# Sixteen weight fetches moved up behind the mixture's branch, the last eight of them on POOL's queue

## The chip, the cores and the metric

One core of a Trainium2 chip runs the whole program in one launch. The metric is device time in microseconds (us), the median of several executions. TensorE is called PE, VectorE DVE, ScalarE ACT, GpSimd POOL and SyncE SP, as in the profile.

## The reference, cut to what matters

Two blocks run one behind the other on 256 tokens of width 1024. The first block has two layers; each is an attention part and then a mixture of experts. The second block (two layers of feed-forward, a three-branch mixer and feed-forward) is untouched by the change. The mixture, with 16 experts of width 1024 and 2 experts per token:

```python
expert, gate = route(h, w_router, b_router)         # 2 of 16 experts for each token
def expert_block(args):
    xblk, e = args
    return (jax.nn.silu(xblk @ w_gate[e]) * (xblk @ w_up[e])) @ w_down[e]
...
y = yb.reshape(n_pad, D) * slot_gate[:, None].astype(h.dtype)
return jnp.zeros_like(h).at[slot_tok].add(y)
```

Everything is fp32. One expert has three 1024 x 1024 matrices of 4 MB, so a layer's mixture reads 16 x 3 x 4 MB = 192 MB of weights, each byte once.

## The kernel before, in words

The mixture is `moe`, called once for each layer. It takes every expert with room for CAP = 64 tokens, two experts (a pair, `pr` = 0 to 7) beside each other in the array. For a pair it forms three products: gate, up and down (`product`, L1883). Between them stand the activation (L1899), the multiplication of gate and up (L1911), eight transposes (L1920), and, behind the down product, four small matmuls for each half that scatter the result back to the tokens (L1951, added up by DVE at L1955).

The weights come in tiles of 1 MB (128 partitions of 8 KB), numbered `n` from 0 to 191 in the order in which they are used: 24 a pair, eight each for gate, up and down. A product has four steps `u`, and a step uses two tiles, one for each expert. `fetch(n)` (L1750) takes a slot from a ring of 16 (`e.wst` with 14 and `wst2` with 2) and issues one DMA on SP's queue (L1762); the last tiles go in smaller parts (L1769, L1776). A tile may be fetched as soon as the tile 16 before it has been used, so the ring always holds the next 16 tiles. The waits are generated, not written: a fetch waits for its slot, and for the landing of an earlier DMA that used the same of SP's completion semaphores.

An expert may get more than 64 tokens. For that there is a general path, `moe_overflow` (L1975), in a branch on the largest count (L1979). Every engine comes past that branch; with these inputs no engine goes into it. It stands in pair 5 behind the transposes, that is ahead of pair 5's down product. Just ahead of it, 16 fetches are issued in a loop (tiles 136 to 151: pair 5's down and pair 6's gate), so that the ring is full when the engines come to the branch. All later fetches are asked for where a product needs its tile (`if i not in loaded: fetch(i)` in `product`).

The order of the instructions on each engine is set by a planner, which takes the program's order as priority and estimates when each instruction could run; it also decides which free slot a tile gets. Nothing from outside is put into the branch.

Behind the branch, the first layer also loads the memory's keys and values of the second layer (`mem_kv`, L1280 and L1285: tiles `mkvT`, `mkv`; 1 MB ahead of the branch, 2 MB behind it), and PE forms them in two groups of 32 matmuls (L1292 and L1299). In the first layer, too, POOL's next instruction behind the branch is the load of the table `rel` for the next attention (L1492). In the second layer `mkp` is reused as the activation's buffer, which is why tiles of that name stand in its rows.

Of the kernel before, what the change touches and what calls it, by code (L numbers as in the profile page):

```python
# [236 lines left out]
def behind(e, tail):  # L237

    st = ExitStack()
    for i in tail:  # L240
        st.enter_context(e.tc.issue_after(i.ins))
    return st
# [1012 lines left out]
def paired(x, k):  # L1255

    return x.rearrange("p (c q j) -> p c j q", q=128, j=2)[:, k // 2, k % 2]
# [467 lines left out]
def moe(e, l, done, kv):  # L1725


    nc, I, tc = e.nc, e.I, e.tc
# [18 lines left out]
             for x in (2 * pr, 2 * pr + 1)]  # L1747
    loaded, turn, slots = {}, [0], e.ring + 2

    def fetch(n, t=None):  # L1750

        w, x, u = tiles[n]
        if t is None:
            t = (e.wst if turn[0] < e.ring else wst2).tile([128, 2048], F32, name="w")
            turn[0] = (turn[0] + 1) % slots
        if n < len(tiles) - 8:
            v = [t[:, :1024], t[:, 1024:]] if not isinstance(t, list) else t
            src = I[w][l, x].rearrange("(u p j) f -> u p (j f)", j=2, p=128)[u]
            if isinstance(t, list):
                e.tail = tuple(nc.sync.dma_start(v[j], src[:, j * D:(j + 1) * D]) for j in range(2))  # L1760
            else:
                e.tail = (nc.sync.dma_start(t, src),)  # L1762
            loaded[n] = v
        else:
            t = t.rearrange("p (j f) -> p j f", j=4)
            src = I[w][l, x].rearrange("(u a p j) (n f) -> n u a p j f", a=2, j=2, p=128, n=2)[u // 2, u % 2]
            loaded[n] = [t[:, j] for j in range(4)]
            if n < len(tiles) - 2:
                e.tail = tuple(nc.sync.dma_start(t[:, 2 * a:2 * a + 2], src[a]) for a in range(2))  # L1769
            else:  # L1770
                pieces.append([(t[:, i], src[i // 2, :, i % 2]) for i in range(4)])
                if len(pieces) == 2:
                    for i in range(4):
                        for q in pieces:
                            with behind(e, e.tail):
                                e.tail = (nc.sync.dma_start(*q[i]),)  # L1776
# [25 lines left out]
    for i in (*range(own), *range(16, 16 + slots - own)):  # L1802
        fetch(i)
# [13 lines left out]
    def gather(q):  # L1817

        pool, tag = (e.early, "early1") if q % 2 else (gp, "xg")
        xg.append(pool.tile([128, KD, 256], F32, name=f"xg{q}", tag=tag))  # L1820
        Pm = [x[:, 4 * q - 4:4 * q] if q else x for x in (P12 if q else P4)]
        for kk in range(4):
            pb = e.bank().rearrange("p (j s) -> p j s", j=2)
            for j in range(2):
                k = 2 * kk + j
                i = 0
                for t in range(2):
                    rhs = Pm[t].rearrange("p a b -> p (a b)")
                    for n in (nh, nl):
                        nc.tensor.matmul(pb[:, j], paired(n[t], k), rhs, start=i == 0, stop=i == 3)  # L1830
                        i += 1
                gain_T(e, (l, 0), k, xg[q][:, k], pb[:, j], kk % 2, e.lnp)
# [18 lines left out]
    def scatter_rows(PgT, q):  # L1851

        for t in range(2):
            Pg = mp.tile([128, 8, CAP], F32, name="Pg")
            for n in range(2):
                c = 2 * q + n
                P = P12[t][:, 4 * c - 4:4 * c] if c else P4[t]
                nc.vector.tensor_mul(Pg[:, 4 * n:4 * n + 4], P.bitcast(F32), bc(gate[:, t, 4 * c:4 * c + 4], 2, CAP))
            pt = e.bank().rearrange("p (a t) -> p a t", a=4)
            for a in range(4):  # L1860
                nc.tensor.transpose(pt[:, a], Pg[:, 2 * a:2 * a + 2].rearrange("p a b -> p (a b)"), e.c["ident"])
            nc.scalar.copy(PgT[:, 4 * q:4 * q + 4, t * 128:(t + 1) * 128], pt)
# [3 lines left out]
    def product(lhs):  # L1866

        pb = [e.bank(), e.bank()]
        for u in range(4):
            ws = []  # L1870
            for _ in range(2):
                ws.append(next(used))
            for i in ws:
                if i not in loaded:
                    fetch(i)
            ws = [loaded[i] for i in ws]
            if len(ws[0]) == 2:
                parts = [(j, 2 * u + j, n, slice(n * 512, (n + 1) * 512)) for j in range(2) for n in range(2)]
            else:
                parts = [(j, 4 * (u % 2) + j, u // 2, slice(0, 512)) for j in range(4)]  # L1880
            for j, k, n, sl in parts:
                for i in range(2):
                    m = nc.tensor.matmul(pb[n][64 * i:64 * i + 64], lhs(k, i), ws[i][j][:, sl],  # L1883
                                         start=k == 0, stop=k == KD - 1, tile_position=(0, 64 * i))
        e.done = m
        return pb

    def warm_silu():
        nc.scalar.activation(act.tile([128, 1], F32, name="warm"), P4[0][:, 0, 0:1].bitcast(F32), AF.Silu)
# [4 lines left out]
    for pr in range(8):  # L1894
        x_e = lambda k, i: xg[pr // 2][:, k, (2 * (pr % 2) + i) * CAP:(2 * (pr % 2) + i + 1) * CAP]
        pg = product(x_e)
        a = e.mkp.rearrange("p i j f -> p (i j f)") if l else gp.tile([128, D], F32, name="a")
        for n in range(2):
            nc.scalar.activation(a[:, n * 512:(n + 1) * 512], pg[n], AF.Silu)  # L1899
        pu = product(x_e)  # L1900
        if pr == 0:
            ext.close()
            lp = R(late, "late")
            PgT = e.early.tile([128, 8, T], F32, name="PgT", tag="early0")
            aT = lp.tile([128, 8, 128], F32, name="aT")
            y = lp.tile([128, D], F32, name="y")
            mid = ExitStack()
            mp = R(mid, "mid")
        for n in range(2):
            sl = slice(n * 512, (n + 1) * 512)  # L1910
            nc.vector.tensor_mul(a[:, sl], pu[n], a[:, sl])  # L1911
        if pr in (1, 3, 5):
            gather(len(xg))
        if pr in (2, 3):
            (residual, lambda: scatter_rows(PgT, 1))[pr - 2]()
        for q in range(2):
            pt = e.bank().rearrange("p (a t) -> p a t", a=4)
            for i in range(4):
                k = 4 * q + i
                nc.tensor.transpose(pt[:, i], paired(a, k), e.c["ident"])  # L1920
            nc.scalar.copy(aT[:, 4 * q:4 * q + 4], pt)
        if pr == 5:
            mid.close()
            for i in range(max(loaded) + 1, max(loaded) + 1 + slots):
                fetch(i)
            if e.overflow:
                moe_overflow(e, l, gate, pos, mi, (nh, nl), y[:CAP], yacc)
                warm_silu()
            if kv:
                more = mem_kv(e, 1, R(mid, "mkv"), halves)  # L1930
            if l:
                first = [R(late, "fw0", 2), *halves]
        had = e.done
        if pr == 7:
            pc = [e.bank() for t in range(2)]
            for t in range(2):
                nc.tensor.matmul(pc[t], e.c["ident"], yacc[t][:, 512:], start=True, stop=False)
        py = product(lambda k, i: aT[:, k, 64 * i:64 * i + 64])
        if pr == 0:
            with behind(e, (had,)):  # L1940
                P12 = place(mp, 4, 16)
                scatter_rows(PgT, 0)
        for n in range(2):
            sl = slice(n * 512, (n + 1) * 512)
            last = pr == 7 and n
            copied = nc.scalar.copy(y[:, sl], py[n])
            if pr == 7 and not n:
                warm(e, AF.Sqrt, copied)
            for t in range(2):
                out = pc[t] if last else e.fbank()  # L1950
                nc.tensor.matmul(out, PgT[:, pr, t * 128:(t + 1) * 128], y[:, sl], start=not last, stop=True)  # L1951
                if pr == 0:
                    nc.vector.tensor_copy(yacc[t][:, sl], out)
                elif not last:
                    nc.vector.tensor_add(yacc[t][:, sl], out, yacc[t][:, sl])  # L1955
                if pr == 7:
                    seen = nc.vector.bn_stats(e.bst[t][:, n], out if last else yacc[t][:, sl])
        if pr in (5, 6) and kv:
            more[pr - 5]()
# [199 lines left out]
```

## Time and profile before

| | before |
|---|---|
| time, median of 3 runs (lowest to highest) | 2625.55 us (2625.09 to 2635.1) |
| the profiled execution's own time | 2628.08 us |
| its span, first to last instruction | 2626.3 us |
| PE busy, share of the span | 97% |
| DVE, ACT, POOL busy | 51%, 39%, 4% |
| bytes moved by DMA | 691.68 MB, mean 263 GB/s |
| of these SP's queue (q1) | 681.40 MB |
| POOL's queue (q0) | 5.70 MB |

All times in the rows are us from the start of the span. The first layer's mixture runs from about 118 to 578 us, the second's from about 700 to 1150 us. "SPq", "POOLq" and "PEldq" are the engines' sequencers; the row of a DMA issue says how long the sequencer was at it, not how long the transfer took.

### The profile page before, as it was taken

What the parts mean: (1) busy time and instruction counts of PE and PEld (TensorE: products, weight loads), DVE (VectorE), ACT (ScalarE), POOL (GpSimd) and SP (SyncE); (2) the same over time, 40 slices, a digit from 0 to 9 for tenths busy, and PEclk for the clock granted to TensorE, in tenths of its full rate; (3) what the DMA queues carried; (4) which work ended last, traced back from release to release, by engine and by line L of the source; (5) the groups of instructions that cost most, each with busy time, mean ns of one, the idle gap of its engine ahead of it and who ended that gap; (6) DMA issues with size and microseconds to landing.
All of it is one profiled execution on the core that took longest, in us unless ns stands there. A gap on an engine that the chain in (4) does not pass through costs nothing.

```text
span 2626.3 us, 43551 instructions
## 1 busy us (share of the span) xinstructions
PE 2544.3 (97%) x17866; PEld 1935.6 (74%) x17866; DVE 1349.1 (51%) x2219; ACT 1031.7 (39%) x1686; POOL 108.4 (4%) x175
## 2 busy tenths in 40 slices
PE   8999998999999998989999999999999999999998
PEld 7734433348634443359999988999999999889998
DVE  6512110027412100055577888765665678887665
ACT  7301100026310100044457654654544576745543
POOL 0000000000000000000000031000000000220000
PEclk9999999999999999999999999999999999999999
DMA  9799999997699999986655643666556555425663
GB/s 350 310 406 421 421 421 411 397 387 279 271 392 421 421 421 393 422 306 190 194 162 164 165 119 123 202 186 186 183 185 194 169 164 163 144 92 175 213 192 121
DMA packets 307205, 691.68 MB, mean 263 GB/s; under 512 B 26208, under 2 KB 229984, under 8 KB 259632
## 3 DMA queue, kind: packets, MB, share of 16 engines
q1 hardware_dynamic: 304976, 681.40, 72.1%
q0 software_dynamic: 976, 5.70, 0.5%
q8 instruction: 145, 2.38, 0.4%
q10 hardware_dynamic: 1040, 1.64, 0.2%
q14 instruction: 68, 0.56, 0.1%
HBM read 684.48 MB, written 4.19 MB: 262 GB/s over the span
## 4 chain that ended last, share of the span: by engine, by line
PE 49%; DMA 5%; DVE 4%; ACT 2%; issue 1%; SPq 0%; DVEq 0%; ACTq 0%
PE sbank L100 23%; PE ubank L100 9%; PE bank L100 9%; PE bank L1883 2%; DVE wlo L230 2%; DMA w<-in_w_up_dram 2%; PE abank L100 1%; DMA w<-in_w_down_dram 1%; DMA w<-in_w_gate_dram 1%; DMA w<-in_ffb_w_in_dram 1%; ACT whi L228 0%; PE abank L610 0%; DMA w<-in_w_in_dram 0%; DMA t<-lscr 0%; PE bank L720 0%
## 5 line engine op out<-in xcount | busy, mean ns | idle before, releaser
L228 ACT CAST whi<-w 128x1024 fp32r<-128x1024 f32 x452 | 472.1, 1053 | 469.8 <-PE sbank L100 202.7
L230 DVE TENSOR_TENSOR wlo<-w,whi 128x1024 fp32r<-128x1024 f32 x452 | 552.2, 1226 | 90.6 <-ACT whi L228 28.4
L1883 PE MATMUL bank<-w,xg 128*64 128x512 f32 x1960 | 483.4, 597 | 6.5 <-DMA w<-in_w_up_dram 6.1
L1883 PEld LDWEIGHTS bank<-w,xg 128*64 128x64 f32 x1960 | 165.0, 136 | 299.8 <-issue 264.6
L100 PE MATMUL sbank<-hh,wlo 128*128 128x256 f32 x1216 | 341.6, 281 | 3.1 <-DVE wlo L230 3.1
L100 PE MATMUL sbank<-hh,whi 128*128 128x256 f32 x1216 | 341.7, 281 | 0.9 <-ACT hh L333 0.9
L100 PE MATMUL sbank<-hl,whi 128*128 128x256 f32 x1216 | 340.0, 280 | 1.7 <-DVE hl L334 1.7
L1883 PE MATMUL bank<-w,aT 128*64 128x512 f32 x1024 | 241.0, 602 | 15.7 <-PEq L1979 12.5
L100 PEld LDWEIGHTS sbank<-hh,wlo 128*128 128x128 f32 x1216 | 229.2, 189 | 6.0 <-DVE wlo L230 4.7
L100 PEld LDWEIGHTS sbank<-hl,whi 128*128 128x128 f32 x1216 | 229.7, 189 | 3.8 <-DVE hl L334 1.9
L100 PEld LDWEIGHTS sbank<-hh,whi 128*128 128x128 f32 x1216 | 229.5, 189 | 4.0 <-issue 2.3
L1883 PEld LDWEIGHTS bank<-w,aT 128*64 128x64 f32 x1024 | 88.1, 138 | 157.7 <-issue 146.1
L100 PE MATMUL ubank<-hh,wlo 128*128 128x256 f32 x704 | 195.6, 278 | 2.1 <-DVE wlo L230 2.1
L100 PE MATMUL ubank<-hh,whi 128*128 128x256 f32 x704 | 195.2, 277 | 0.0
L100 PE MATMUL ubank<-hl,whi 128*128 128x256 f32 x704 | 195.1, 277 | 0.0
L100 PE MATMUL bank<-al,whi 128*128 128x256 f32 x704 | 189.7, 278 | 1.0 <-DVE al L342 1.0
L100 PE MATMUL bank<-ah,wlo 128*128 128x256 f32 x704 | 189.7, 277 | 0.0
L1955 DVE TENSOR_TENSOR xn<-fbank,xn 128x512 f32<-128x512 f32 x52 | 35.9, 691 | 280.8 <-PE fbank L1951 280.8
L100 PE MATMUL bank<-ah,whi 128*128 128x256 f32 x704 | 176.1, 278 | 0.5 <-ACT ah L341 0.3
L100 PE MATMUL sbank<-whi,hl 128*128 128x256 f32 x512 | 144.8, 283 | 0.0
L100 PE MATMUL sbank<-wlo,hh 128*128 128x256 f32 x512 | 144.6, 283 | 0.0
L100 PE MATMUL sbank<-whi,hh 128*128 128x256 f32 x512 | 143.5, 282 | 0.0
(525 smaller groups left out, 4486.6 us busy)
## 6 DMA issues: line engine op xcount, KB each, us to landing
w<-in_w_gate_dram SPq DMA_DIRECT2D x128, 1024.0 KB, 19.8
w<-in_w_up_dram SPq DMA_DIRECT2D x117, 1024.0 KB, 19.8
w<-in_w_down_dram SPq DMA_DIRECT2D x112, 1024.0 KB, 19.8
w<-in_w_in_dram SPq DMA_DIRECT2D x140, 512.0 KB, 3.6
w<-in_ffa_w_in_dram SPq DMA_DIRECT2D x88, 512.0 KB, 4.7
w<-in_ffb_w_in_dram SPq DMA_DIRECT2D x88, 512.0 KB, 4.7
w<-in_ffa_w_out_dram SPq DMA_DIRECT2D x44, 512.0 KB, 4.2
w<-in_ffb_w_out_dram SPq DMA_DIRECT2D x44, 512.0 KB, 4.3
```

The lines of the kernel that those rows point to most:

```text
L100: m = nc.tensor.matmul(out, a, b, start=first and i == 0, stop=last and i == 2, skip_group_check=skip)
L228: c = nc.scalar.copy(hi, w)
L230: m = nc.vector.tensor_sub(lo, w, hi.bitcast(F32))
L1883: m = nc.tensor.matmul(pb[n][64 * i:64 * i + 64], lhs(k, i), ws[i][j][:, sl], start=k == 0, stop=k == KD - 1, tile_position=(0, 64 * i))
L1955: nc.vector.tensor_add(yacc[t][:, sl], out, yacc[t][:, sl])
```

## The change: what it does

`fetch` gets an argument `queue`, SP's by default, for the tiles that go in one DMA. Behind the branch, and ahead of `mem_kv`, a loop now asks for the next 16 tiles at once. After the 16 ahead of the branch these are tiles 152 to 167: the first eight (pair 6's up tiles) on SP's queue, the second eight (pair 6's down tiles) on POOL's queue. Both layers run it. Each of the 16 still waits for its slot, which is that of a tile of pair 5's down (for 152 to 159) or pair 6's gate (for 160 to 167). Tiles from 168 on are fetched as before.

```diff
-    def fetch(n, t=None):
+    def fetch(n, t=None, queue=nc.sync):
...
-                e.tail = (nc.sync.dma_start(t, src),)
+                e.tail = (queue.dma_start(t, src),)
...
             if e.overflow:
                 moe_overflow(e, l, gate, pos, mi, (nh, nl), y[:CAP], yacc)
                 warm_silu()
+                for i in range(16):
+                    fetch(max(loaded) + 1, queue=nc.gpsimd if i >= 8 else nc.sync)
             if kv:
```

## Rows read from the trace of the kernel before

**Rows 1.** The page: 40 slices of the span, DMA share in tenths and rate.
```profile
DMA  9799999997699999986655643666556555425663
GB/s 350 310 406 421 421 421 411 397 387 279 271 392 421 421 421 393 422 306 190 194 162 164 165 119 123 202 186 186 183 185 194 169 164 163 144 92 175 213 192 121
```

**Rows 2.** Stretches about both branches: length, busy of the engines, clock, DMA, GB/s.
```profile
457.00:464.00 7.00, 7.00 (x36) 2.82 (x33) 0.00 (x0) 0.00 (x0) 0.00 (x0) 1.00 0.33 127
1035.00:1042.00 7.00, 7.00 (x34) 2.76 (x32) 0.00 (x0) 0.00 (x0) 0.00 (x0) 1.00 0.47 159
1000.00:1025.00 25.00, 18.70 (x78) 7.73 (x77) 1.38 (x2) 1.17 (x2) 0.00 (x0) 0.86 1.02 419
```

**Rows 3.** SP's issues in order, both branches: start, time to the last issue, tile, count.
```profile
428.30 14.27 SPq L1762 DMA_DIRECT2D w<-in_w_gate_dram  x6
461.36 0.93 SPq L1285 DMA_DIRECT2D mkv<-in_w_mem_k_dram  x2
463.48 6.23 SPq L1762 DMA_DIRECT2D w<-in_w_up_dram  x8
...
1001.87 17.77 SPq L1762 DMA_DIRECT2D w<-in_w_gate_dram  x8
1039.42 4.17 SPq L1762 DMA_DIRECT2D w<-in_w_up_dram  x8
```

**Rows 4.** The branch's line on each sequencer: duration ns min/median/max, first and last start.
```profile
L1979 SPq EVENT_SEMAPHORE  x16: 17/17/17, 458.3 to 1039.3; - x16
L1979 POOLq COMPARE_BRANCH  x2: 45/45/45, 115.2 to 697.2; - x2
L1979 PEldq COMPARE_BRANCH  x2: 6007/6048/6088, 423.4 to 1004.3; - x2
```

**Rows 5.** PE in order, second layer, pairs 5 to 7: start, us, operation, count, wait before.
```profile
1010.75 15.35 PE L1883 MATMUL bank<-w,aT 128*64 128x512 f32 x64 [6.16 <-PEq L1979]
...
1063.00 3.65 PE L1883 MATMUL bank<-w,xg 128*64 128x512 f32 x12 [0.55 <-DMA w<-in_w_up_dram]
...
1082.89 3.65 PE L1883 MATMUL bank<-w,aT 128*64 128x512 f32 x12 [0.56 <-DMA w<-in_w_down_dram]
1086.46 1.98 PE L1951 MATMUL fbank<-y,PgT 128*128 128x512 f32 x4
...
1092.15 15.09 PE L1883 MATMUL bank<-w,xg 128*64 128x512 f32 x64
...
1126.31 1.60 PE L1920 MATMUL bank<-ident,mkp 128*128 128x128 f32 x8
```

**Rows 6.** The same for the first layer.
```profile
452.51 13.95 PE L1883 MATMUL bank<-w,xg 128*64 128x512 f32 x60
466.39 7.17 PE L1292 MATMUL fbank<-mkvT,mkv 128*128 128x256 f32 x32
...
510.43 3.65 PE L1883 MATMUL bank<-w,aT 128*64 128x512 f32 x12 [0.55 <-DMA w<-in_w_down_dram]
514.01 1.98 PE L1951 MATMUL fbank<-y,PgT 128*128 128x512 f32 x4
...
530.38 24.73 PE L1883 MATMUL bank<-w,xg 128*64 128x512 f32 x112
```

**Rows 7.** DMA queues in 535 to 536 us: packets, MB, share of the 16 engines.
```profile
q1 hardware_dynamic: 32, 0.25, 60.2%
q0 software_dynamic: 25, 0.15, 37.7%
```

**Rows 8.** POOL in order, 500 to 600 us.
```profile
531.03 0.58 POOL L1492 DMA_DIRECT2D rel<-in_dtab_dram  x1 [419.45 <-PE fbank L1299]
```

**Rows 9.** DMA issues: queue, count, KB of each, median us from issue to landing.
```profile
w<-in_w_gate_dram SPq DMA_DIRECT2D x128, 1024.0 KB, 19.8
rel<-in_dtab_dram POOLq DMA_DIRECT2D x1, 384.0 KB, 8.0
```

## The prediction

> **What bounds the kernel now.** I read the slices first. While the mixtures run, DMA is full at about 421 GB/s (slices 4 to 6 and 13 to 17) [rows 1]; a 1 MB tile (1.049 MB) then takes 2.49 us. Where one slice of a mixture falls short, 1 us stretches led to the two branches. There DMA runs dry: 7 us at a mean of 127 GB/s in the first layer and 159 in the second [rows 2], that is 7 x (421 - 127) / 421 = 4.9 us and 7 x (421 - 159) / 421 = 4.4 us of transfer lost.
>
> SP's order shows why. It finishes issuing pair 6's gate tiles at 442.57 (428.30 + 14.27) and issues nothing until 461.36; in the second layer it pauses from 1019.64 to 1039.42 [rows 3]. The slots for the next tiles are free long before: pair 5's down product begins at 1010.75 and takes 15.35 us [rows 5]. What holds SP is the branch's line, with eight semaphore waits in each layer, the last at 1039.3 [rows 4]: it waits until everything in flight has landed. POOL has nothing in flight and passes the same branch at 115.2 and 697.2 [rows 4].
>
> Then PE's order. Behind the branches PE waits for tiles in the second layer from pair 6's up product on, ending with a step at 1063.00 for the last up tile and one at 1082.89 for the last down tile [rows 5]. In the first layer the step at 510.43 is the last that waits for DMA [rows 6]; after it PE is the bound to the layer's end, because `mem_kv` gave it 14.3 us more work (twice 7.17 [rows 6]) in the same stretch.
>
> **The change part by part.**
>
> *Moved on SP.* Tiles 152 to 159 are already SP's next fetches behind the branch, and they are still stuck there. Asking earlier gains nothing. In the first layer they may pass `mem_kv`'s 2 MB; I take the old order (memory loads first), as those loads wait for no slot of the ring and SP issues them ahead today [rows 3]; the other order is a rival.
>
> *Moved to POOL.* Eight issues leave SP. SP takes 0.52 us for one (4.17 us for eight [rows 3]) and POOL 0.58 [rows 8], beside 2.49 us of transfer, so the issuing costs and saves nothing on the path. What counts is when the tiles start and what they take. POOL waits for its slots alone. In the second layer pair 6's gate product runs in steps of 16 matmuls; its long run gives 15.09 / 64 = 0.236 us a matmul [rows 5]. In the first layer its last 60 begin at 452.51, so its first two slots come free about 12 x 0.236 = 2.8 us later, at 455.3; in the second layer the same step ends about 1034.5, an estimate from the first layer's distances. Nothing stands behind the eight on POOL that could suffer: the next is `rel`, at 531.03 [rows 8], 60 us after the last gate tile is used. POOL's one load in a full stretch was issued at 531.03 [rows 8] and is moving at 535 [rows 7]; with 2 to 3 us of start (an estimate from these) down tiles move in the gap from about 457.5 and 1037. Most of the lost 4.9 and 4.4 us is recovered **as transfer time**.
>
> *What it costs.* The tiles in the gap are the wrong ones: down tiles, while PE needs the up tiles next. And once SP is back, both queues are full. How they share is shown by `rel`: in 535 to 536 POOL's queue moved 25 packets and SP's 32, with 37.7% and 60.2% of the engines' time [rows 7]. POOL's packets were smaller there (0.15 / 25 = 6 KB against 8 KB); with 8 KB on both sides POOL gets about 25 / 57 = 44%. It also landed in 8.0 us where SP's fetches take 19.8, eight tiles deep [rows 9], so it doesn't stand behind them.
>
> *Second layer.* Before, the eight up tiles moved alone and the down tiles followed. Now at 1041, when SP's bytes flow again, POOL has moved about 1.4 of its eight tiles (the gap, less what the gate tiles' remains take). The eight up tiles at 56% take 8 x 2.49 / 0.56 = 35.6 us and land by 1041 + 35.6 + 0.6 = 1077.2 (0.6 for completion, an estimate). The down tiles are there by 1082.9 - 4.4 = 1078.5. So PE's last up step starts at 1077.2, not 1063.00: 14 us late. From there it has its tiles: the step 3.65, transposes 1.6, down 14.9 (64 matmuls at 0.233, 13.95 / 60 [rows 6]), which ends at 1097.3 against 1086.46 [rows 5]. Then the slack pays back. From 1086.46 to 1126.31 PE took 39.85 us; without waiting, the scatter and gate take 1092.15 + 15.09 x 60 / 64 - 1086.46 = 19.8 and up 14.9, together 34.7 [rows 5]. That recovers 5.1. What is left, 10.8 - 5.1 = **+5.7 us**, goes to the end, as the last down product was PE's own pace before too.
>
> *First layer.* SP has ten tiles in its queue (2 MB of memory weights and the eight up tiles), so the up tiles are the last of all to land: by 510.4 - 4.9 = 505.5. Then 505.5 + 3.65 + 1.5 + 14.9 = 525.5, where the scatter began at 514.01 [rows 6]: 11.5 late. Nothing pays back, since PE didn't wait for DMA after 510.43 (112 matmuls in 24.73, 0.221 each [rows 6]). **+11.5 us**. DMA finishes earlier than PE in both layers now, and its gain ends as slack.
>
> *Sum.* 11.5 + 5.7 = 17.2 us. On the profiled execution 2628.08 + 17.2 = 2645.3; that one lies 2.5 above the median, so the forecast is 2625.55 + 17.2 = 2642.8, say 2643.
>
> *Unknown prices.* POOL's share with many 1 MB tiles in its queue isn't shown; from both sides, a third (the up tiles come sooner, the sum about +10) and a quarter (the down tiles become the late ones: at 10 us a tile 66 us, to about 1107, some +20 a layer). I take 44%, the nearest row. PE's new waits are four of 4 to 6 us a layer; after one of 6.16 the stretch from 1000 to 1025 was granted 0.86 [rows 2, 5], that is, part of it at the lower level, 1.2 GHz. Most of that falls under the next wait; bounds are 0 and 3.65 us a layer (the last step at half pace). The planner may lay out other instructions anew, either way; I take 0.
>
> **A rule that speaks against all this.** POOL's load passed SP's queue, 8.0 us against 19.8 [rows 9]. The Trainium skill, "DMA: Bandwidth & Descriptors", section "Issuing engines are not separate DMA queues", says that DMAs of all issuing engines run and interleave on the same 16 DMA engines, and that issuing from several saves only the sequencer's time. By it alone the sum would be nothing, as the issue time is hidden. Both agree that bandwidth isn't added; but order and the moment of the start change, which the rows show and the sentence leaves out.
>
> **The rivals.**
>
> 1. *The gap is filled and the order does no harm* (not slower). If POOL's packets took only what SP leaves, the up tiles would keep their pace while the down tiles start in the gap. Then all lands 4.9 and 4.4 us sooner, and both layers end that much earlier: 2625.55 - 9.3 = 2616. It is decided by POOL's share while SP's queue is full; from about nothing, with the down tiles still in time, it wins. For it: the gap is real [rows 2]. Against: 37.7% in the one stretch that shows it [rows 7].
> 2. *A milder share*, about a third: +10, 2635.5.
> 3. *The memory loads fall behind the up tiles* in the first layer, while PE's keys (L1292) stay ahead of the up product [rows 6]. Then 18 tiles must land first, about 506, and keys 7.2, up 14.9, transposes 1.5, down 14.9 end at 544.5 against 514.01: +30.5 there, +36 in all, 2662. Against: today's order [rows 3].
> 4. *Nothing*: POOL's fetches come so late (the planner puts them behind something, or their slots are the last to be given) that they go in the old order. 2625.5.
>
> **How the numbers follow.** Forecast 0.52 (its own range 2634 to 2653), rival 1 0.12, rival 2 0.14, rival 3 (with the quarter share) 0.12, rival 4 0.10. About 0.5%, 13.1 us, can be told from no change. Slower by more: 0.46 of the forecast, all of rival 3: 0.58. Faster by more needs rival 1 and a planner's gift of 4 us: 0.04. The rest is 0.38. The range goes from rival 1 to rival 3, 2616 to 2662.
>
> **What would show it.** Right: no dry 7 us at the branches (over 300 GB/s there); eight POOL issues a layer from about 455 and 1034, two for each gate step, landing in 20 us or more; up tiles about 4.5 us apart; PE's last up step of pair 6 some 14 us later, its down product with no wait for DMA; the layers' ends later by about 11 and 6. Wrong: up steps at the old times with POOL's tiles in flight (rival 1), or PE waiting for down tiles (POOL's share is small). The forecast fails if PE's slack behind the late up tiles is larger than the rows say.

## The result, and the profile after

The changed kernel takes 2652.55 us in the median of 8 runs (2640.67 to 2658.82) and the kernel before, timed beside it, 2630.89 (8 runs). The ratio is 1.0089 with a 95% interval of 1.007 to 1.0108, that is +23 us (18 to 28). The profiled execution took 2650.35 us, its span is 2648.6.

The two dry stretches are gone. The windows of the changed kernel, with the columns of [rows 2]; the first two are the stretches that ran dry before (they lie 4 us earlier and 8 us later here), the other two lie behind them:

```profile
453.00:460.00 7.00, 7.00 (x36) 2.87 (x35) 0.00 (x0) 0.00 (x0) 2.17 (x5) 1.00 1.00 408
1043.00:1050.00 7.00, 7.00 (x35) 2.77 (x32) 0.00 (x0) 0.00 (x0) 2.30 (x5) 1.00 0.97 386
...
464.00:476.00 12.00, 2.10 (x5) 1.77 (x6) 0.00 (x0) 0.00 (x0) 0.00 (x0) 0.55 1.02 418
...
1050.00:1075.00 25.00, 16.34 (x38) 4.37 (x36) 0.00 (x0) 1.19 (x2) 1.97 (x4) 0.75 1.01 423
```

408 and 386 GB/s stand where 127 and 159 stood [rows 2]. DMA is now nearly full there (a share of 1.00 and 0.97), but in the next stretches PE is busy for 2.10 of 12 us and 16.34 of 25, at a granted clock of 0.55 and 0.75: it waits, and it falls to 1.2 GHz for a part of the time.

What fills the gaps are POOL's issues, two for each step of pair 6's gate product. POOL in order (start, us, and in brackets the wait before; some of the issues are left out):

```profile
451.68 0.58 POOL L1762 DMA_DIRECT2D w<-in_w_down_dram  x1 [342.85 <-PE bank L1883]
...
462.92 0.53 POOL L1762 DMA_DIRECT2D w<-in_w_down_dram  x1 [0.27 <-issue]
538.15 0.54 POOL L1492 DMA_DIRECT2D rel<-in_dtab_dram  x1 [74.71 <-DMA w<-in_w_up_dram]
...
1042.99 0.55 POOL L1762 DMA_DIRECT2D w<-in_w_down_dram  x1 [341.19 <-PE bank L1883]
1043.84 0.55 POOL L1762 DMA_DIRECT2D w<-in_w_down_dram  x1 [0.29 <-issue]
...
1054.13 0.53 POOL L1762 DMA_DIRECT2D w<-in_w_down_dram  x1 [0.29 <-issue]
```

SP's order around the branches answers to [rows 3]; it is held up as before, from 438.68 (424.48 + 14.20) to 458.79 and from 1027.72 to 1047.48:

```profile
424.48 14.20 SPq L1762 DMA_DIRECT2D w<-in_w_gate_dram  x6
458.79 0.95 SPq L1285 DMA_DIRECT2D mkv<-in_w_mem_k_dram  x2
459.79 9.87 SPq L1285 DMA_DIRECT2D mkv<-in_w_mem_v_dram  x2
469.75 12.71 SPq L1762 DMA_DIRECT2D w<-in_w_up_dram  x8
...
1009.95 17.77 SPq L1762 DMA_DIRECT2D w<-in_w_gate_dram  x8
1047.48 3.88 SPq L1762 DMA_DIRECT2D w<-in_w_up_dram  x8
```

From 1048 on both queues are full. Their packets, MB and shares of the 16 engines from 1052 to 1072, in the second layer:

```profile
q0 software_dynamic: 580, 4.22, 50.6%
q1 hardware_dynamic: 579, 4.23, 50.5%
```

POOL's queue (q0) and SP's (q1) each moved half, packet for packet. In these 20 us half of the rate went to tiles that nobody needed yet. PE in the second layer shows who paid (as [rows 5]; the scatter's line is now L1953):

```profile
1034.09 1.98 PE L1953 MATMUL fbank<-y,PgT 128*128 128x512 f32 x4
...
1057.16 3.67 PE L1883 MATMUL bank<-w,xg 128*64 128x512 f32 x4 [3.44 <-DMA w<-in_w_up_dram]
...
1073.56 6.91 PE L1883 MATMUL bank<-w,xg 128*64 128x512 f32 x16 [3.04 <-DMA w<-in_w_up_dram]
...
1087.07 3.65 PE L1883 MATMUL bank<-w,xg 128*64 128x512 f32 x12 [0.55 <-DMA w<-in_w_up_dram]
...
1092.24 14.00 PE L1883 MATMUL bank<-w,aT 128*64 128x512 f32 x64
1106.18 1.98 PE L1953 MATMUL fbank<-y,PgT 128*128 128x512 f32 x4
...
1111.87 27.68 PE L1883 MATMUL bank<-w,xg 128*64 128x512 f32 x124
...
1160.39 1.98 PE L1953 MATMUL bank<-y,PgT 128*128 128x512 f32 x4 [0.73 <-ACT y L1948]
```

The reader is to see three things: waits of up to 3.4 us ahead of the up steps, where before they were 0.6; then 64 down matmuls in one run (14.00) with no wait, since these tiles had come early; then 124 matmuls of gate and up in one run, where before the up product waited. From its wait at 1087.07 on PE waits for no tile up to the layer's end.

To compare stages, all kernels are laid on one mark: the first scatter of pair 5, the first thing behind the branch that neither the fetches nor the memory loads touch. Its row and that of the last scatter, in the trace of the kernel before, both layers:

```profile
446.82 1.98 PE L1951 MATMUL fbank<-y,PgT 128*128 128x512 f32 x4
...
575.95 1.98 PE L1951 MATMUL bank<-y,PgT 128*128 128x512 f32 x4 [0.73 <-ACT y L1946]
...
1026.03 1.98 PE L1951 MATMUL fbank<-y,PgT 128*128 128x512 f32 x4
...
1147.16 1.98 PE L1951 MATMUL bank<-y,PgT 128*128 128x512 f32 x4 [0.73 <-ACT y L1946]
```

From mark to last scatter this gives 129.13 us in the first layer and 121.13 in the second. The changed kernel needs 139.69 (442.87 to 582.56) and 126.30: **+10.6 and +5.2 us**. All kernels of this study, from one profile each (the experiments follow below; sp16, which does the work of before, shows by its -1.5 how far a layer can be off by chance):

| kernel | time against before, ratio (95%) | first layer, mark to end | second layer | last scatter to the span's end |
|---|---|---|---|---|
| before | | 129.13 | 121.13 | 1479.1 |
| changed | 1.0089 (1.007 to 1.0108) | +10.6 | +5.2 | 1488.2 |
| sp16 | 1.0004 (0.9984 to 1.0023) | +0.4 | -1.5 | 1478.7 |
| pool2 | 0.9981 (0.9964 to 0.9998) | -3.3 | -3.9 | 1482.4 |
| pool4 | 0.9987 (0.9969 to 1.0004) | +0.6 | -3.9 | 1471.4 |
| swap | 1.0021 (1.0004 to 1.0038) | +7.1 | -2.8 | 1487.2 |
| mix | 1.0103 (1.0071 to 1.0135) | +12.0 | +6.2 | 1490.5 |
| l0only | 1.0043 (1.0026 to 1.006) | +10.4 | -0.2 | 1472.5 |
| l1only | 1.0028 (1.0012 to 1.0045) | 0.0 | +5.2 | 1494.6 |

### The profile page after: what moved, and what is told of

The parts are those of the page before. It is cut to its first block, busy times and chain, and to the rows that moved or that the text cites. A ratio compares the mean times of both kernels' runs of the same rounds, so it can differ in the third digit from the quotient of the medians.

```text
span 2648.6 us, 43573 instructions
## 1 busy us (share of the span) xinstructions
PE 2557.8 (97%) x17866; PEld 1953.8 (74%) x17866; DVE 1349.3 (51%) x2219; ACT 1030.1 (39%) x1686; POOL 116.0 (4%) x191
## 4 chain that ended last, share of the span: by engine, by line
PE 50%; DVE 5%; DMA 3%; ACT 2%; issue 1%; SPq 0%; DVEq 0%; ACTq 0%
PE sbank L100 23%; PE ubank L100 9%; PE bank L100 9%; PE bank L1883 3%; DVE wlo L230 2%; DMA w<-in_w_up_dram 1%; PE abank L100 1%; ACT whi L228 1%; DMA w<-in_w_in_dram 0%; DMA t<-lscr 0%; PE fbank L1953 0%; PE bank L786 0%; DMA w<-in_ffb_w_in_dram 0%; PE bank L720 0%; PE bank L776 0%
## 5 line engine op out<-in xcount | busy, mean ns | idle before, releaser
L1883 PE MATMUL bank<-w,aT 128*64 128x512 f32 x1024 | 234.7, 603 | 13.0 <-PEq L1981 12.5
```

## The experiments

All start from the changed kernel. The theory: POOL's tiles fill the gap, but their order is wrong, and the up tiles lose half the rate. Two rivals: A, asking early moves other work, whatever the queue; B, a tile through POOL's queue is dear in itself.

**sp16: all on SP's queue.**

```diff
-                    fetch(max(loaded) + 1, queue=nc.gpsimd if i >= 8 else nc.sync)
+                    fetch(max(loaded) + 1)
```

> All 16 tiles behind the branch are asked for early, all on SP's queue. My theory (the up tiles lose half the transfer rate to down tiles that are needed later): nothing changes, the dry gap of 7 us at each branch is back, the time is that of before within 0.2%. Rival A (asking early moves other work, whatever the queue): about +20 us, as in the changed kernel. Rival B (a tile through POOL's queue is dear in itself, 1.4 us for each of the 16): nothing, as no tile goes there.

Measured: 1.0004. The gap is back, and SP's order is that of before. Its windows at the branches:

```profile
454.00:461.00 7.00, 7.00 (x36) 2.88 (x35) 0.00 (x0) 0.00 (x0) 0.00 (x0) 1.00 0.39 129
1034.00:1041.00 7.00, 7.00 (x36) 2.87 (x34) 0.00 (x0) 0.00 (x0) 0.00 (x0) 1.00 0.52 187
```

Asking early does nothing by itself; rival A is out.

**pool2 and pool4: two and four of the second eight on POOL's queue.**

```diff
-                    fetch(max(loaded) + 1, queue=nc.gpsimd if i >= 8 else nc.sync)
+                    fetch(max(loaded) + 1, queue=nc.gpsimd if 8 <= i < 10 else nc.sync)     # pool2
...
+                    fetch(max(loaded) + 1, queue=nc.gpsimd if 8 <= i < 12 else nc.sync)     # pool4
```

> Only the first two of the second eight (tiles 160 and 161) go through POOL's queue, the other six behind the up tiles on SP's. My theory: the two tiles run in the gap (about 1.6 of them fit), the up tiles lose under 1 us, and the down tiles and all behind them come 4 to 5 us sooner in each layer: 8 us faster than before (-0.3%), with 300 GB/s or more in the gap. Rival A: about +20 us. Rival B: 4 tiles x 1.4 = +5 us.

> The first four of the second eight go through POOL's queue. My theory: gap filled, then 2.4 tiles share the rate with the up tiles, whose last lands about 5 us late: nothing gained in the first layer, 4 us in the second, -4 us in all (-0.15%). Rival A: about +20 us. Rival B: 8 tiles x 1.4 = +11 us.

Measured: 0.9981 (-5 us, 0.5 to 9) and 0.9987 (-3 us, with no change inside the interval). Layer by layer pool2 won 3.3 and 3.9; pool4 won 3.9 in the second and nothing in the first, as expected (its 0.6 is within what one profile can be off). So two tiles through POOL's queue win, four lose nothing, and rival B, which has every one of them cost and forecast +5 and +11, is out. pool2 is faster than the changed kernel, and than the kernel before by an interval that just excludes no change; 8 us were expected, 7.2 are seen inside the layers and 5 in the time. Its windows at the branches, and PE in its second layer:

```profile
457.00:464.00 7.00, 7.00 (x34) 2.77 (x32) 0.00 (x0) 0.00 (x0) 0.55 (x1) 1.00 0.97 397
1032.00:1039.00 7.00, 7.00 (x36) 2.81 (x33) 0.00 (x0) 0.00 (x0) 1.06 (x2) 1.00 0.95 378
```

```profile
1023.15 1.98 PE L1953 MATMUL fbank<-y,PgT 128*128 128x512 f32 x4
...
1061.21 3.65 PE L1883 MATMUL bank<-w,xg 128*64 128x512 f32 x12 [0.54 <-DMA w<-in_w_up_dram]
1064.86 1.60 PE L1920 MATMUL bank<-ident,mkp 128*128 128x128 f32 x8
1066.38 14.01 PE L1883 MATMUL bank<-w,aT 128*64 128x512 f32 x64
1080.32 1.98 PE L1953 MATMUL fbank<-y,PgT 128*128 128x512 f32 x4
```

The gaps are filled (397 and 378 GB/s). The last up step comes 38.06 us behind the mark, where before it was 36.97 (1063.00 [rows 5] less 1026.03): 1 us late. The pair's next scatter comes 57.17 behind it, against 60.43 before (1086.46 less 1026.03): 3.3 us early.

**swap: the up tiles on POOL's queue, the down tiles on SP's.**

```diff
-                    fetch(max(loaded) + 1, queue=nc.gpsimd if i >= 8 else nc.sync)
+                    fetch(max(loaded) + 1, queue=nc.gpsimd if i < 8 else nc.sync)
```

> The first eight (the up tiles) go through POOL's queue, the second eight through SP's. Slots of the up tiles are free as soon as pair 5's down product runs, so POOL sends them while pair 6's gate tiles are still under way. My theory: both share the rate, the gate tiles land some 18 us late, the gate product ends 15 us late, the up product finds its tiles there, and the down product ends about 6 us late; the second layer has 5 us of slack for that: +6 and +1, together +7 us (+0.3%). If the order of need alone decided (up tiles ahead of down tiles do no harm): -9 us. Rival B: 16 x 1.4 = +22 us.

Measured: 1.0021 (+6 us, 1 to 10); the layers +7.1 and -2.8. The order of the tiles is right here, but POOL's up tiles, whose slots are free at once, take their share from the gate tiles. PE's longest wait in the first layer, and the queues from 445 to 455:

```profile
464.94 11.86 PE L1883 MATMUL bank<-w,xg 128*64 128x512 f32 x36 [11.98 <-DMA w<-in_w_gate_dram]
```

```profile
q0 software_dynamic: 503, 3.67, 87.3%
q1 hardware_dynamic: 503, 0.52, 14.9%
```

SP is then at the load of `mkvT`, in packets of 1 KB (0.52 MB / 503), with the gate tiles behind it, so POOL takes not half but seven eighths of the bytes; in the second layer, without that load, it is 435 packets to 434 from 1030 to 1045. That the first layer loses was expected in sign and size. The second was expected at +1 and won 2.8. Its trace shows where the difference lies: pair 6's scatter comes 64.15 us behind the mark (1095.54 less 1031.39) against 60.43 before, 3.7 late where 6 were expected, and from there to the last scatter 6.5 us are won back where 5 were reckoned with.

**mix: the order of the changed kernel, on SP's queue alone.**

```diff
-                for i in range(16):
-                    fetch(max(loaded) + 1, queue=nc.gpsimd if i >= 8 else nc.sync)
+                b = max(loaded) + 1
+                for i in range(16):
+                    fetch(b + i // 2 + 8 * (i % 2))
```

> All 16 tiles on SP's queue, in the order up, down, up, down (152, 160, 153, 161, ...), which is the order that an even share of two queues makes. POOL issues none of them. My theory (the loss is the order alone): the gap is there as before, the last up tile lands as the 15th of 16, the up product ends some 17 us late, the pair's down product then runs without a wait and ends 14 us late in both layers, the second layer wins 5 back: 14 + 9 = +23 us, about as much as the changed kernel's +22. If POOL's queue is what costs (its start, its descriptors, its packets): no more than +5 us.

Measured: 1.0103 (+27 us, 19 to 36); the layers +12.0 and +6.2, where 14 and 9 were expected. No tile goes through POOL, the gaps are there, and the loss is about that of the changed kernel. Its windows at the branches, and PE in its second layer:

```profile
453.00:460.00 7.00, 7.00 (x36) 2.90 (x35) 0.00 (x0) 0.00 (x0) 0.00 (x0) 1.00 0.32 121
1043.00:1050.00 7.00, 7.00 (x36) 2.89 (x35) 0.00 (x0) 0.00 (x0) 0.00 (x0) 1.00 0.55 200
```

```profile
1058.53 6.89 PE L1883 MATMUL bank<-w,xg 128*64 128x512 f32 x16 [2.46 <-DMA w<-in_w_up_dram]
1069.74 6.90 PE L1883 MATMUL bank<-w,xg 128*64 128x512 f32 x16 [4.31 <-DMA w<-in_w_up_dram]
1079.68 6.90 PE L1883 MATMUL bank<-w,xg 128*64 128x512 f32 x16 [3.04 <-DMA w<-in_w_up_dram]
1089.63 5.34 PE L1883 MATMUL bank<-w,xg 128*64 128x512 f32 x12 [3.04 <-DMA w<-in_w_up_dram]
...
1096.50 13.95 PE L1883 MATMUL bank<-w,aT 128*64 128x512 f32 x64
```

The same picture as in the changed kernel: waits at every up step, then a down product in one run. This order makes such a loss without POOL's queue. One thing differs besides: PE's order is laid out a little differently here, with 22 matmuls of the next gate product ahead of pair 6's scatter.

**l0only and l1only: the change in one layer.**

```diff
-                    fetch(max(loaded) + 1, queue=nc.gpsimd if i >= 8 else nc.sync)
+                    fetch(max(loaded) + 1, queue=nc.gpsimd if i >= 8 and l == 0 else nc.sync)     # l0only
...
+                    fetch(max(loaded) + 1, queue=nc.gpsimd if i >= 8 and l == 1 else nc.sync)     # l1only
```

> The changed kernel in the first layer; in the second all 16 tiles go through SP's queue. My theory: +11 us from the first layer, which has no slack behind pair 6, and nothing in the second. If the loss were the same in both layers: +11 us too, and then l1only also +11; if a part of the measured +22 arises behind the mixtures, the sum of the two runs stays below 22: l0only +11, l1only +5, sum 16.

> The changed kernel in the second layer only. My theory: +5 us, since 5 us of PE's former waits for the last up product take up a part of the 11 us delay. If there is no such slack: +11 us.

Measured: 1.0043 (+11 us, 7 to 16) and 1.0028 (+7 us, 3 to 12). Inside the layers it is +10.4 and -0.2 in one kernel, 0.0 and +5.2 in the other: each part is there without the other, and at the size forecast for it.

## Why the prediction was right

*The gap and its cause.* Right: SP is still held at the branch, POOL isn't, and its tiles moved in the gap. Their issues begin at 451.68 and 1042.99, which is 8.81 and 8.90 us behind the mark. The forecast had the first slots free at 455.3 and 1034.5, 8.5 behind it. One sign was off: POOL's tiles were to take 20 us or more to land, and took 6.8 to 28.9, with a median of 12.8.

*The share.* Sized at 44%, measured 50.6% in the second layer. The step forecast for the last up tile was 51.2 us behind the mark (1077.2 less 1026.03) and came at 52.98 (1087.07 less 1034.09). The forecast hardly hung on this term once it was near a half: at 50% POOL's 6.6 tiles left would be through first, and the up tiles would land when all 14.6 tiles have, after 36.4 us (14.6 x 2.49) and not 35.6.

*Second layer.* The pair's down product was to end 10.8 us late and the layer 5.7. It ended 72.09 us behind the mark (1106.18 less 1034.09) against 60.43, 11.7 late, and the layer 5.2 late. So 6.5 us were paid back where 5.1 were forecast; the slack is the run of 124 matmuls without a wait. The price of the lower clock was left between 0 and 3.65 us. It was nothing here: a step behind a long wait took 6.91 us for 16 matmuls, where a step before took 4.41, but the last step ran at full pace again (12 in 3.65).

*First layer.* The end was right: +10.6 where 11.5 was forecast, with almost nothing paid back. The way there was not. Four waits of 4 to 6 us at the up steps were forecast; there was one long wait, ahead of the memory's keys (as [rows 6]):

```profile
448.56 13.95 PE L1883 MATMUL bank<-w,xg 128*64 128x512 f32 x60
473.90 3.75 PE L1292 MATMUL fbank<-mkvT,mkv 128*128 128x256 f32 x8 [11.39 <-issue]
479.68 8.46 PE L1292 MATMUL fbank<-mkvT,mkv 128*128 128x256 f32 x24 [2.02 <-DMA mkv<-in_w_mem_k_dram]
...
502.00 3.65 PE L1883 MATMUL bank<-w,xg 128*64 128x512 f32 x12 [0.55 <-DMA w<-in_w_up_dram]
505.58 1.60 PE L1920 MATMUL bank<-ident,a 128*128 128x128 f32 x8
507.11 14.00 PE L1883 MATMUL bank<-w,aT 128*64 128x512 f32 x64
521.04 1.98 PE L1953 MATMUL fbank<-y,PgT 128*128 128x512 f32 x4
```

The view names no releaser for the 11.39 us ("issue"). That they too are a wait for the weights of the keys is inferred: these weights were issued from 458.79 on, the memory's four loads took 15.0 to 21.7 us to land, and 458.79 + 15.0 is 473.8. The queues from 464 to 472 show why they were late:

```profile
q0 software_dynamic: 407, 2.96, 87.9%
q1 hardware_dynamic: 407, 0.42, 14.8%
```

407 packets on each side, but SP's are those of the memory loads, of 1 KB (0.42 MB / 407), and POOL's of 7.3 KB on average (2.96 / 407). So SP got an eighth of the bytes there, not half. POOL's tiles were through by about 480. The forecast reckoned all SP's bytes at one share. That it came out at the same place says nothing for its way: it had to, since the up tiles were the last to land either way and DMA was full throughout: the last up step at 502.00 is 59.1 us behind the mark, and 58.7 was forecast (505.5 less 446.82).

*The sum.* 17.2 us forecast, 15.7 inside the layers, +23 (18 to 28) in the time. In the profiled execution the whole is 22.3: -3.95 up to the first mark, +10.6, +1.4 between the layers, +5.2, and +9.1 behind the last scatter. That last part is code which the change doesn't touch; in all nine profiles it has 12644 instructions on PE, 1665 on DVE and 1237 on ACT, at a granted clock of 0.99 or 1.00. In the nine profiles it takes 1471.4 to 1494.6 us, and not in the order of the kernels: l0only is the second shortest, l1only the longest. One profile's 9.1 can't be laid to the change. The times of l0only and l1only add up to 11 + 7 = 18, at the lower edge of the interval. Taking from each kernel's time (the ratio's part of the time before) what its two layers show leaves about 8 us in the changed kernel and 9 in mix, and 0 to 2 in the other six. That looks like more than chance, but with one profile of each kernel no run shows where it arises: the account covers some 16 of the 23 us, and the rest is open.

*The rule on issuing engines.* By the sentence of the Trainium skill that is cited ahead of the result, taken alone, the time was to stay. It didn't: to add no bandwidth is not to change nothing. The packet counts, 580 to 579 and 407 to 407, agree with another section of the same page of the Trainium skill, "DMA: Bandwidth & Descriptors", "Queues, rings and completion order", by which each DMA engine goes round between the queues that have work, one packet at a time. (The counts can't tell how many of the profile's packets go at a turn.)

*The rivals.* Rival 1 named what decides, POOL's share while SP's queue is full, and the share was half. The gain that rival 1 forecast (9.3 us) is there once the dose is small, but not because POOL's packets give way: pool2 won 7.2 us inside the layers with two tiles that about fit in the hole. Rivals 3 and 4 didn't happen; the memory loads kept their place ahead of the up tiles, though they landed late all the same, by way of the packets.

## What to carry to other kernels

Here a second queue was a way round a stalled first one, and didn't wait behind it; what it carried took its share at once, wanted or not. Put there only as much as fits in the hole (here two tiles of 1 MB for a hole of 4 to 5 us), and ask what the transfers that are needed next lose. To see whether a loss is the order or the queue, make the same order on the old queue.

## What the runs showed of the hardware that was not expected

Two full queues shared by packets, not by bytes: with about 7.3 KB in the mean packet on both sides 50.6% and 50.5% of the engines' time, with about 7.3 KB against 1 KB 87.9% and 14.8%, and in swap 87.3% and 14.9%. A load in short packets was starved by a load in long ones on another queue: the memory's loads took 20.7 us to land in the median, where they took 5.2 before.

The stretch behind the mixtures, the same work in every kernel, differs by 23 us among the nine profiles, as much as the whole effect measured.
